# Triangular inverses from blocks of 16, with one more merging level, in a two-layer flow-matching step

## The chip, the cores and the metric

The kernel runs on one core of one Trainium2 chip. The metric is the device time of one launch in microseconds, the median of several runs. A core has five engines with queues of their own: TensorE for matrix products (PE in the rows, PEld its weight loads), VectorE (DVE), ScalarE (ACT), GpSimd (POOL), and SyncE (SP), which here only issues DMAs. Each engine takes its instructions strictly in the order in which the program emits them.

## The reference

Two layers, with the same weights for both streams, run over 128 context tokens and 256 latent tokens (T = 384 in all, width 1024). A layer mixes tokens by a gated DeltaNet (8 heads, both directions), a gated short convolution, and grouped-query attention, then applies an MLP with a hidden width of 4096. The part that matters here is the DeltaNet solve. For every head and direction a unit lower triangular matrix is inverted (or solved against) per chunk:

```python
diff = gc[..., :, None] - gc[..., None, :]
decay = jnp.where(incl, jnp.exp(jnp.where(incl, diff, 0.0)), 0.0)
kb = kc * bc[..., None]
m = jnp.where(strict, jnp.einsum("nbhid,nbhjd->nbhij", kb, kc) * decay, 0.0)
a = m + jnp.eye(C, dtype=f32)
u = lax.linalg.triangular_solve(a, vc * bc[..., None], left_side=True, lower=True)
w = lax.linalg.triangular_solve(a, kb * jnp.exp(gc)[..., None], left_side=True, lower=True)
```

Everything else of a layer is matrix products with float32 weights, norms, gates and softmax.

## The kernel before

**Products.** Each weight block is split into a high and a low part in a reduced float32 type (`wh` by ScalarE, `wl` by VectorE), and each large product runs as three passes (hi·hi, hi·lo, lo·hi), 128x384 or 128x512 at a time, into PSUM tiles named `mm`. Small float32 products go to PSUM tiles named `ax`; the trace records each of those as two instructions, one after the other.

**The inverses (`delta_a`, line 1304).** For one head the kernel forms six 128x128 triangular matrices `M` (two directions, three blocks of 128 tokens). It inverts the 32x32 diagonal blocks of all six at once by substitution on VectorE: 31 steps of a shuffle (`MB<-Mc`), a product (`Pr<-MB,Xc`) and a reduction (`Xc<-Pr`), each step longer than the last. Two levels of block merging on TensorE then give the 128x128 inverse `xe`: 12 products of 32x32 (`ax<-xe,M`), 18 of 32x32 (`ax<-NT`), 6 and 6 of 64x64. These use a part of the array each, so that several can run at once; the text calls them tiled products, and a row of them with nothing else between a run. `delta_b` (line 1433) then uses `xe`. There are 8 heads in each of two layers, so 16 inversions in all.

**The start.** The first layer's modulation vectors come from small products on weights that stream in (`ax<-ws,csil`), a norm needs the column sums of squares (`ax<-sel,sq`), and the first three-pass products follow as soon as the first two blocks of the normed input are there. Products of a matrix of ones with itself (`mm<-ones`, called fillers) stand on TensorE where the planner expects it to idle.

**What sets the order.** The program is first recorded, and `schedule` (line 239) then plans it: each instruction gets a cost from `cost` (line 180) and a priority from its class, and a greedy list scheduler writes the order of every engine. `tiled` (line 162) marks tiled products; leaving tiled mode costs `SWITCH` in the plan. A running balance `bal` of TensorE's work against the share `BUSY` decides on fillers that stand before work that is ready; other fillers fill the plan's idle time. The plan's durations only set the order. On the chip each instruction runs when its engine reaches it and its inputs are there.

Of the kernel before, what the change touches and what calls it, by code (L numbers as in the profile page):

```python
# [9 lines left out]
F32 = mybir.dt.float32  # L10
# [3 lines left out]
AX = mybir.AxisListType  # L14
ADD, SUB, MUL = ALU.add, ALU.subtract, ALU.mult

P = 128
# [144 lines left out]

def tiled(op, ins):

    return "tile_position" in op.k or (op.kind == "matmul" and ins[0].ap[0][1] < P)


def shared_port(op, method, outs, ins, tag):
# [11 lines left out]
def cost(op, method, outs, ins, tag):  # L180

    n = max(size(v) for v in outs[:1] + ins)
    ps = any(tag.get(v.tensor.name) in PSUM_TAGS for v in outs + ins)
    if op.eng == "PE":
        n = size(outs[0])
        if tiled(op, ins):
            if "tile_position" in op.k:
                return n * 0.965 + 3 if op.k["tile_position"] == (0, 0) else 27.0
            return 43.0 if n <= 32 else 71.0
        if method == "transpose":  # L190
            return n * 2 / 2.4 + 3
        if ins[0].dtype == F32R and n >= 256:
            return n / 2.4 + 13.8
        return max(214.0, n * 4 / 2.4 + 3)
    if op.eng == "ACT":
        c = 51 + n * 0.833 + (0 if ps else 42)
        c += 93 * sum(isap(op.k.get(x)) for x in ("bias", "scale")) + 93 * (method == "mul")
        return c + (93 if "accum_out" in op.k else 0)
    if op.eng == "DVE":
        if method == "reciprocal":  # L200
            return 69 + 6.25 * n
        fast = method in ("tensor_scalar", "tensor_copy") and not ps
        sc = sum(isap(op.k.get(x)) for x in ("scalar", "scalar1", "scalar2"))
        return 69 + n * 1.042 * (0.5 if fast else 1) + 58 * sc
    if op.eng == "POOL":
        if method == "memset":
            return 35 + n * 0.833
        if method == "affine_select":
            return 160 + n * 0.83
        if method == "tensor_copy":  # L210
            return 250 if n <= 96 else 345
        return (165 + n * 2.1) if op.k.get("op") != ALU.pow else 300 + 165 * n
    return max(56.0, n * outs[0].shape[0] * 4 / 385.0)
# [15 lines left out]


WINDOW = 3413.0
SWITCH = 63.0
FILL_MARGIN = 100.0
BUSY = 0.4
CREDIT = 600.0
URGENT = {"crit": 1, "step": 1, "crit2": 1, "step2": 1}


def schedule(rec, par):
# [48 lines left out]
            enable(o)  # L288
    for tg in list(queue):
        grant(tg)  # L290
    done, mode = 0, False
    port = bal = last = 0.0
    order = []
    while done < len(ops):
        best = None
        for e in engs:
            t = now[e]
            while future[e] and future[e][0][0] <= t:
                r, p, i = heapq.heappop(future[e])
                heapq.heappush(avail[e], (p, i))  # L300
            if avail[e]:
                c = (t, e)
            elif future[e]:
                c = (future[e][0][0], e)
# [5 lines left out]
        t, e = best  # L310
# [7 lines left out]
        if e == "PE" and warm and warm[0].end is not None:  # L318

            f = warm[0]  # L320
            while True:
                t0 = pe_end
                c = f.cost * slowness(t0)
                if t0 < f.end or t0 + c > t - FILL_MARGIN:
                    break
                g = copy.copy(f)
                g.start, g.end, g.i = t0, t0 + c, o.i
                order.append(g)
                win[1] += g.stream
                bal = min(CREDIT, bal + f.stream * (1 - BUSY))  # L330
                pe_end = t0 + c
            if bal < 0 and o.stream < 0.5 * o.cost and t < par["thin"] and f.end <= t:

                t0 = max(pe_end, t)
                g = copy.copy(f)
                g.start, g.end, g.i = t0, t0 + f.cost * slowness(t0), o.i
                order.append(g)
                win[1] += g.stream
                bal += f.stream * (1 - BUSY)
                now[e] = pe_end = g.end  # L340
                heapq.heappush(avail[e], (p, i))
                continue
# [22 lines left out]
        if e == "SP":  # L365
            if len(flight) >= 8:
                t = o.start = max(t, flight[-8] + 908)
            hw = max(t, hw) + 475
            now[e] = hw - 25
            dma = max(dma, hw + 1800) + o.cost  # L370
            o.end = dma
            flight.append(dma)
        else:
            c = o.cost * slow
            if o.port:
                c += max(0.0, port - t)
                port = t + c
            if e == "PE":
                c += SWITCH * slow * (mode and not o.tiled)
                mode = o.tiled  # L380
                pe_end = t + c
                if o.cls == "fill":
                    o.end = t + c
                    warm.append(o)
                elif warm and warm[0].last is o:
                    warm.pop(0)
                bal = min(CREDIT, bal + o.stream - BUSY * (t + c - last))
                last = t + c
                win[1] += o.stream
            o.end = now[e] = t + c  # L390
# [47 lines left out]
def build(tc, aps):  # L438
# [23 lines left out]
    def axtile():  # L462
        return pax.tile([P, 512], F32, tag="ax", name="ax")
# [6 lines left out]
    sel2 = const.tile([P, 2], F32, name="sel2")  # L470
    sel = const.tile([P, 3, 3], F32, name="sel")
    delta = const.tile([P, 2, 32], F32, name="delta")
    rc = const.tile([P, 2, P], F32, name="rc")
    rs = const.tile([P, 2, P], F32, name="rs")
    mhalf = const.tile([P, 1], F32, name="mhalf")
# [152 lines left out]
    def X(fn, *a):  # L628
        items.append(((), lambda _: fn(*a)))
# [146 lines left out]
    def late_consts():  # L776
        for t_, n_ in ((cdn, "cdn"), (utri, "utri"), (ltri, "ltri"), (delta, "delta"), (rc, "rc"), (rs, "rs"),
                       (csc, "csc"), (gdn, "gdn"), (gqc, "gqc")):
            SP.dma_start(t_, aps[n_])
        for t_, n_ in ((alog, "alog"), (dtb, "dtb")):  # L780
            SP.dma_start(t_, aps[n_].partition_broadcast(P))


    def modfinish(l, pieces, sums):
# [340 lines left out]
    def layer(l):  # L1125
# [178 lines left out]
        def delta_a(h):  # L1304
# [42 lines left out]
                DVE.tensor_tensor(out=E[:, d].rearrange("p t f -> p (t f)"), in0=pq[:, :T],  # L1347
                                  in1=E[:, d].rearrange("p t f -> p (t f)"), op=MUL)
            yield
            Mc, Pr = (W(n, [2, 3, 32]) for n in ("Mc", "Pr"))  # L1350
            Xc = W("Xc", [2, 3, 32], 2)
            Mr = W("Mr", [3, 32])
            for q in range(4):
                s = slice(32 * q, 32 * q + 32)
                POOL.tensor_copy(Mr[s, :, ::-1], M[s, 1, :, s])
            for q in range(4):
                s = slice(32 * q, 32 * q + 32)
                POOL.tensor_copy(Mc[s, 0], M[s, 0, :, s])

            DVE.stream_shuffle(out=Mc[:, 1], in_=Mr, mask=list(range(31, -1, -1)))  # L1360
            POOL.tensor_copy(Pr, delta.unsqueeze(2).to_broadcast([P, 2, 3, 32]))
            DVE.tensor_copy(Xc[:, :, :, 0], delta[:, :, 0:1].to_broadcast([P, 2, 3]))
            yield
            for d in range(2):

# [2 lines left out]
                                   pattern=[[0, 3], [sg, P]], channel_multiplier=-sg)  # L1368
            yield
            f6 = lambda v: v.rearrange("p d t c -> p (d t) c")  # L1370
            for i in range(1, 32):
                MB = W("MB", [2, 3, 32], 2)
                DVE.stream_shuffle(out=f6(MB)[:, :, 0:i], in_=f6(Mc)[:, :, 0:i], mask=[i] * 32)
                DVE.tensor_tensor(out=f6(Pr)[:, :, 0:i], in0=f6(MB)[:, :, 0:i], in1=f6(Xc)[:, :, 0:i], op=MUL)
                DVE.tensor_reduce(out=f6(Xc)[:, :, i], in_=f6(Pr)[:, :, 0:i + 1], axis=AX.X, op=ADD)
                yield

            nt = W("NT", [2, 3, P]).rearrange("p d t f -> p (d t f)")
            U1, U2, Xn, Xh = (nt[:, a:b].rearrange("p (t f) -> p t f", t=n)
                              for a, b, n in ((0, 96, 3), (96, 288, 3), (288, 480, 6), (480, 672, 3)))  # L1380
            DVE.transpose(Xn[:, 0:3], Xc[:, 0])
            DVE.transpose(Xn[:, 3:6], Xc[:, 1, :, ::-1])
            Q = [slice(32 * q, 32 * q + 32) for q in range(4)]
            POOL.memset(Xh[Q[0], :, 32:64], 0.0)
            POOL.memset(Xh[Q[3], :, 0:32], 0.0)
            for q in range(4):
# [3 lines left out]
                yield  # L1390
            for d in range(2):
                for q in range(4):
                    POOL.tensor_copy(xe[Q[q], d, :, Q[q]], Xc[Q[q], d, :, ::-1] if d else Xc[Q[q], d])
            yield
            p1 = axtile()
            p1a = p1[:, 0:96].rearrange("p (t f) -> p t f", t=3)
# [269 lines left out]
        if l == 0:  # L1666
            X(warmup)
            X(pre0)
            evacs = [evac_qkv(0, w) for w in (1, 0, 2)] + [evac_mg(f, True) for f in range(3)]
            for q in range(4):  # L1670
                mq = modquarter(q)
                items.extend(mq[:3])
                if q == 0:
                    X(early_consts)
                items.extend(mq[3:])
                for k in (2 * q, 2 * q + 1):
                    X(lambda k=k: make_h(k))
                    if q < 3:
                        X(lambda k=k: norm_x(k + 2))
                if q == 3:  # L1680
                    X(hold)
                    X(late_consts)
                items.extend(firstproducts(q, evacs))
            X(lambda: save_x(om))
        m2 = modlist(l, "B") if l else []
# [265 lines left out]
```

## Time and profile before

| | |
|---|---|
| median of 3 runs | 1961.99 us (1960.59 to 1962.01) |
| the profiled execution | 1958.58 us |
| its span, first to last instruction | 1957.0 us |
| TensorE busy | 1944.6 us (99%) |
| VectorE busy | 1425.2 us (73%) |
| ScalarE busy | 946.1 us (48%) |
| GpSimd busy | 395.9 us (20%) |
| granted TensorE clock, mean | 1.000 |

TensorE's instructions overlap: a 128x384 pass has a duration of about 341 ns in the rows, and the next starts about 174 ns after it. So the distance between two starts tells what a product costs, and the durations do not.

### The profile page before, as it was taken

What the parts mean: (1) busy time and instruction counts of PE and PEld (TensorE: products, weight loads), DVE (VectorE), ACT (ScalarE), POOL (GpSimd) and SP (SyncE); (2) the same over time, 40 slices, a digit from 0 to 9 for tenths busy, and PEclk for the clock granted to TensorE, in tenths of its full rate; (3) what the DMA queues carried; (4) which work ended last, traced back from release to release, by engine and by line L of the source; (5) the groups of instructions that cost most, each with busy time, mean ns of one, the idle gap of its engine ahead of it and who ended that gap; (6) DMA issues with size and microseconds to landing.
All of it is one profiled execution on the core that took longest, in us unless ns stands there. A gap on an engine that the chain in (4) does not pass through costs nothing.

```text
span 1957.0 us, 35787 instructions
## 1 busy us (share of the span) xinstructions
PE 1944.6 (99%) x12938; PEld 1800.1 (92%) x12938; DVE 1425.2 (73%) x4354; ACT 946.1 (48%) x2176; POOL 395.9 (20%) x651
## 2 busy tenths in 40 slices
PE   9999999999999999999999999999999999999998
PEld 7998999999999899789789999999999998898987
DVE  4688899988869688879467989779888645533334
ACT  3566555555433354334246665545554434543432
POOL 0122122222222312013011022222132212110210
PEclk9999999999999999999999999999999999999999
DMA  8532233333336846866554233333333334544352
GB/s 281 176 105 84 99 121 123 117 116 116 109 114 224 288 142 215 236 207 207 158 183 148 76 97 115 116 119 127 117 116 109 112 129 151 199 124 129 127 126 71
DMA packets 133713, 280.40 MB, mean 143 GB/s; under 512 B 11904, under 2 KB 82080, under 8 KB 133536
## 3 DMA queue, kind: packets, MB, share of 16 engines
q1 hardware_dynamic: 133536, 278.12, 43.9%
q8 instruction: 102, 1.67, 0.3%
q14 instruction: 75, 0.61, 0.1%
HBM read 270.66 MB, written 7.42 MB: 142 GB/s over the span
## 4 chain that ended last, share of the span: by engine, by line
PE 92%; DVE 3%; DMA 2%; ACT 1%; issue 1%; POOL 0%; DVEq 0%; ACTq 0%; POOLq 0%
PE mm L1855 77%; PE ax L1855 15%; DMA wr<-in_wmod 1%; DMA wr<-in_wf 1%; DVE macc L1855 1%; DVE wl L1855 1%; ACT wh L1855 0%; DVE q L1855 0%; DVE XT L1855 0%; ACT junk L1855 0%; ACT E L1855 0%; ACT mm L1855 0%; DVE qu L1855 0%; DVE ns L1855 0%; ACT ht L1855 0%
## 5 line engine op out<-in xcount | busy, mean ns | idle before, releaser
L1855 DVE TENSOR_TENSOR wl<-wr,wh 128x1024 fp32r<-128x1024 f32 (+2 forms) x382 | 480.3, 1259 | 295.6 <-ACT wh L1855 289.6
L1855 ACT CAST wh<-wr 128x1024 fp32r<-128x1024 f32 (+2 forms) x382 | 396.3, 1038 | 564.3 <-PE mm L1855 438.0
L1855 PE MATMUL mm<-HL,wh 128*128 128x384 f32 x1648 | 561.8, 341 | 0.0
L1855 PE MATMUL mm<-HH,wh 128*128 128x384 f32 x1648 | 561.4, 341 | 0.0
L1855 PE MATMUL mm<-HH,wl 128*128 128x384 f32 x1648 | 559.5, 340 | 0.0
L1855 PEld LDWEIGHTS mm<-HL,wh 128*128 128x128 f32 x1648 | 309.7, 188 | 6.0 <-issue 3.1
L1855 PEld LDWEIGHTS mm<-HH,wh 128*128 128x128 f32 x1648 | 309.5, 188 | 6.1 <-issue 3.7
L1855 PEld LDWEIGHTS mm<-HH,wl 128*128 128x128 f32 x1648 | 309.8, 188 | 5.3 <-issue 3.3
L1855 DVE SCALAR_TENSOR_TENSOR macc<-wr,csil,macc 128x1024 f32<-128x1024 f32 x98 | 141.3, 1478 | 12.5 <-DMA wr<-in_wmod 12.5
L1855 PE MATMUL mm<-wh,HL 128*128 128x256 f32 (+1 forms) x480 | 140.6, 293 | 0.0
L1855 PE MATMUL mm<-wh,HH 128*128 128x256 f32 (+1 forms) x480 | 138.9, 290 | 1.3 <-DVE k_y L1855 0.7
L1855 PE MATMUL mm<-wl,HH 128*128 128x256 f32 (+1 forms) x480 | 139.9, 292 | 0.2 <-DVE wl L1855 0.2
L1855 DVE TENSOR_TENSOR Pr<-MB,Xc 128x6 f32<-128x6 f32 (+30 forms) x496 | 138.7, 280 | 0.2
L1855 DVE TENSOR_REDUCE Xc<-Pr 128x6 f32<-128x12 f32 (+30 forms) x496 | 127.1, 256 | 8.1
L1855 DVE STREAM_SHUFFLE MB<-Mc 128x6 f32<-128x6 f32 (+30 forms) x496 | 132.0, 271 | 0.0
L1855 PE MATMUL mm<-al,wh 128*128 128x384 f32 x384 | 130.7, 340 | 0.0
L1855 PE MATMUL mm<-ah,wl 128*128 128x384 f32 x384 | 130.5, 340 | 0.0
L1855 PE MATMUL mm<-ah,wh 128*128 128x384 f32 x384 | 130.0, 339 | 0.0
L1855 PE MATMUL mm<-wh,u 128*128 128x512 f32 x384 | 122.7, 396 | 0.0
L1855 PE MATMUL mm<-wh,ah 128*128 128x512 f32 x288 | 112.9, 392 | 0.0
L1855 PE MATMUL mm<-wl,ah 128*128 128x512 f32 x288 | 112.6, 391 | 0.0
L1855 PE MATMUL mm<-wh,al 128*128 128x512 f32 x288 | 112.6, 391 | 0.0
(278 smaller groups left out, 3304.1 us busy)
## 6 DMA issues: line engine op xcount, KB each, us to landing
wr<-in_wf SPq DMA_DIRECT2D x330, 512.0 KB, 3.3
wr<-in_wmod SPq DMA_DIRECT2D x80, 512.0 KB, 4.3
wr<-in_wq SPq DMA_DIRECT2D x16, 512.0 KB, 3.2
wr<-in_wdg SPq DMA_DIRECT2D x16, 512.0 KB, 3.3
ws<-in_wmod SPq DMA_DIRECT2D x16, 384.0 KB, 6.4
E<-scr SPq DMA_DIRECT2D x16, 384.0 KB, 3.7
Qe<-scr SPq DMA_DIRECT2D x16, 256.0 KB, 3.9
wr<-in_wkv SPq DMA_DIRECT2D x8, 408.0 KB, 3.9
```

The source lines that it names most:

```text
L1855: o.call(*o.a, **o.k)
```

## The change

Substitution stops at blocks of 16: 15 steps instead of 31. Each 32x32 block is now held as two 16x16 blocks stacked on the partitions, picked by two masks `hsel`. One more level of merging on TensorE puts two inverses of 16 together into one of 32: 24 products of 32x32, a copy by ScalarE, 24 more, and an addition on VectorE; all operands lie in a new tile `Rp`. In the planner the costs of tiled products and of leaving tiled mode get new numbers, told apart by the kind of tiled product, and the balance behind fillers is kept against a share of 0.2 instead of 0.4.

```diff
 def tiled(op, ins):
-    return "tile_position" in op.k or (op.kind == "matmul" and ins[0].ap[0][1] < P)
+    return 1 if "tile_position" in op.k else 2 if op.kind == "matmul" and ins[0].ap[0][1] < P else 0
...
-            return 43.0 if n <= 32 else 71.0
+            return 11.0 if n <= 32 else 42.0
...
-SWITCH = 63.0
+SWITCH = {0: 0.0, 1: 63.0, 2: 190.0}
 BUSY = 0.4
+THIN = 0.2
...
-                bal = min(CREDIT, bal + f.stream * (1 - BUSY))
+                bal = min(CREDIT, bal + f.stream * (1 - THIN))
...
-                c += SWITCH * slow * (mode and not o.tiled)
+                c += 0.0 if o.tiled else SWITCH[mode] * slow
...
-                bal = min(CREDIT, bal + o.stream - BUSY * (t + c - last))
+                bal = min(CREDIT, bal + o.stream - THIN * (t + c - last))
...
-            Mc, Pr = (W(n, [2, 3, 32]) for n in ("Mc", "Pr"))
+            rp = W("Rp", [4, 192])
+            F, D, N, Dn = (rp[:, j].rearrange("p (d t c) -> p d t c", d=2, t=3) for j in range(4))
+            Mc, Pr, Xs = (W(n, [2, 3, 16]) for n in ("Mc", "Pr", "Xs"))
...
+            for d in (1, 0):
+                DVE.tensor_scalar(out=Pr[:, d], in0=F[:, d, :, 16:32], scalar1=m1, scalar2=None, op0=MUL)
+                x, y, z = F[:, d, :, 0:16], Pr[:, d], Mr if d else Mc[:, 0]
+                if d:
+                    x, y = x[:, :, ::-1], y[:, :, ::-1]
+                DVE.scalar_tensor_tensor(out=z, in0=x, scalar=m0, in1=y, op0=MUL, op1=ADD)
...
-            for i in range(1, 32):
-                MB = W("MB", [2, 3, 32], 2)
-                DVE.stream_shuffle(out=f6(MB)[:, :, 0:i], in_=f6(Mc)[:, :, 0:i], mask=[i] * 32)
...
+            for i in range(1, 16):
+                MB = W("MB", [2, 3, 16], 2)
+                DVE.stream_shuffle(out=f6(MB)[:, :, 0:i], in_=f6(Mc)[:, :, 0:i], mask=[i] * 16 + [16 + i] * 16)
...
+            for d in range(2):
+                x = Xs[:, d, :, ::-1] if d else Xs[:, d]
+                for b, m in enumerate((m0, m1)):
+                    DVE.tensor_scalar(out=D[:, d, :, 16 * b:16 * b + 16], in0=x, scalar1=m, scalar2=None, op0=MUL)
+            for d in range(2):
+                DVE.transpose(Dn[:, d], D[:, d])
...
+                        PE.matmul(p0a[Q[q], d, t], lhsT=N[Q[q], d, t], rhs=D[Q[q], d, t], start=True, stop=True)
+            ACT.copy(F, p0a)
...
+                        PE.matmul(p0b[Q[q], d, t], lhsT=Dn[Q[q], d, t], rhs=F[Q[q], d, t], start=True, stop=True)
+            DVE.tensor_tensor(out=Xc, in0=p0b, in1=D, op=ADD)
```

On TensorE in the start of the program, before, after the first blocks of the input have been turned (`mm<-ident,XT`), the nine small products for the norm stand one by one between fillers (`mm<-ones`):

```order
L1855 MATMUL mm<-ident,XT 128x128 x2
L1855 MATMUL mm<-ones 128x128 x5
L1855 MATMUL ax<-sel,sq 128x3
L1855 MATMUL mm<-ones 128x128 x5
L1855 MATMUL ax<-sel,sq 128x3
L1855 MATMUL mm<-ones 128x128 x4
L1855 MATMUL ax<-sel,sq 128x3
```

In the changed kernel the same place on TensorE, to the broadcast of the norm (`ax<-ident,np_y`), reads:

```order
L1896 MATMUL mm<-ident,XT 128x128 x2
L1896 MATMUL mm<-ones 128x128
L1896 MATMUL ax<-sel,sq 128x3 x3
L1896 MATMUL mm<-ident,XT 128x128 x2
L1896 MATMUL ax<-sel,sq 128x3 x3
L1896 MATMUL ax<-ws,csil 32x256
L1896 MATMUL ax<-sel,sq 128x3 x3
L1896 MATMUL ax<-ws,csil 32x256 x7
L1896 MATMUL mm<-ident,XT 128x128 x8
L1896 MATMUL ax<-ws,csil 32x256 x3
L1896 MATMUL mm<-ones 128x128 x2
L1896 MATMUL ax<-ident,np_y 128x128 x3
```

The norm's products have moved ahead and modulation products stand among them. Up to the first three-pass product the program now has 34 fillers instead of 56; all later stages keep theirs.

On TensorE in the first head's inversion, the changed kernel has the new level between passes of a weight block (`mm<-HH,wh` and so on) and an attention product (`ax<-KTA,OT`):

```order
L1896 MATMUL mm<-HL,wh 128x384
L1896 MATMUL ax<-Rp 32x32 x12
L1896 MATMUL mm<-HH,wl 128x384
L1896 MATMUL ax<-Rp 32x32 x12
L1896 MATMUL ax<-KTA,OT 128x384
L1896 MATMUL mm<-HH,wh 128x384
L1896 MATMUL ax<-Rp 32x32 x24
L1896 MATMUL mm<-HL,wh 128x384
```

All eight heads of both layers look alike (in one the first 24 stand as 8 and 16, in one the last 24 as 11 and 13). The later levels keep their runs, so that a head has nine runs of tiled products where it had six: 145 runs of 32x32 and 64x64 products in the whole program where it had 98, and 1248 products of 32x32 where it had 480. No other kind of product on TensorE changes its number, but for the fillers.

## Rows read from the trace of the kernel before

**Rows 1.** The page: busy time, share of the span and instructions of each engine.

```profile
PE 1944.6 (99%) x12938; PEld 1800.1 (92%) x12938; DVE 1425.2 (73%) x4354; ACT 946.1 (48%) x2176; POOL 395.9 (20%) x651
```

**Rows 2.** Waits of TensorE: what waited for whom; us in total, times, longest.

```profile
PE ax L1855 <- DVE macc L1855: 2.5, 2, 2.0
PE ax L1855 <- DVE q L1855: 1.1, 3, 0.4
PE mm L1855 <- POOL sel L1855: 1.1, 1, 1.1
PE mm L1855 <- DVE k_y L1855: 0.7, 1, 0.7
PE mm L1855 <- DVE kn L1855: 0.6, 1, 0.6
```

**Rows 3.** Both mixer stages: length, busy per engine, clock, DMA share, GB/s.

```profile
96.00:665.00 569.00, 567.73 (x4162) 541.77 (x4162) 489.70 (x1802) 301.34 (x780) 143.57 (x262) 1.00 0.38 128
...
1041.00:1630.00 589.00, 588.28 (x4283) 566.20 (x4283) 467.73 (x1789) 315.86 (x817) 131.44 (x262) 1.00 0.34 114
```

**Rows 4.** TensorE in order of time, one tiled product: start, us, what, records.

```profile
234.28 0.34 PE L1855 MATMUL mm<-ah,wh 128*128 128x384 f32 x1
...
234.80 0.34 PE L1855 MATMUL mm<-ah,wh 128*128 128x384 f32 x1
235.07 0.24 PE L1855 MATMUL ax<-xe,M 32*32 32x32 f32 x2
235.24 0.44 PE L1855 MATMUL mm<-al,wh 128*128 128x384 f32 x1
235.52 0.34 PE L1855 MATMUL mm<-ah,wl 128*128 128x384 f32 x1
235.70 0.34 PE L1855 MATMUL mm<-ah,wh 128*128 128x384 f32 x1
```

**Rows 5.** The same view of TensorE, a run of 18 tiled products.

```profile
239.38 0.34 PE L1855 MATMUL mm<-al,wh 128*128 128x384 f32 x1
239.65 0.52 PE L1855 MATMUL ax<-NT 32*32 32x32 f32 x36
240.10 0.44 PE L1855 MATMUL mm<-ah,wl 128*128 128x384 f32 x1
240.37 0.34 PE L1855 MATMUL mm<-ah,wh 128*128 128x384 f32 x1
240.55 0.34 PE L1855 MATMUL mm<-al,wh 128*128 128x384 f32 x1
```

**Rows 6.** The same view of TensorE, the start of the program.

```profile
10.56 1.28 PE L1855 MATMUL mm<-ones 128*128 128x128 f32 x10
11.68 0.28 PE L1855 MATMUL ax<-sel,sq 128*128 128x3 f32 x2
...
18.60 0.28 PE L1855 MATMUL ax<-sel,sq 128*128 128x3 f32 x2
...
27.57 0.59 PE L1855 MATMUL mm<-HH,wh 128*128 128x384 f32 x2
```

**Rows 7.** VectorE in order of time, the start of the program.

```profile
11.92 0.56 DVE L1855 TENSOR_TENSOR sq<-sq 128x384 f32<-128x384 f32 x1 [0.27 <-ACT sq L1855]
...
18.92 0.16 DVE L1855 TENSOR_SCALAR n_sx<-ax 128x3 f32<-128x3 f32 x1 [1.23 <-PE ax L1855]
```

**Rows 8.** The start in a stretch of 5 us, columns as in Rows 3.

```profile
15.00:20.00 5.00, 5.00 (x41) 4.37 (x40) 1.12 (x2) 1.66 (x2) 0.83 (x1) 1.00 1.09 364
```

**Rows 9.** Groups of VectorE, the substitution: count, busy us, mean ns, idle before.

```profile
L1855 DVE TENSOR_TENSOR Pr<-MB,Xc 128x6 f32<-128x6 f32 (+30 forms) x496 | 138.7, 280 | 0.2
L1855 DVE STREAM_SHUFFLE MB<-Mc 128x6 f32<-128x6 f32 (+30 forms) x496 | 132.0, 271 | 0.0
L1855 DVE TENSOR_REDUCE Xc<-Pr 128x6 f32<-128x12 f32 (+30 forms) x496 | 127.1, 256 | 8.1
```

**Rows 10.** Groups of ScalarE and VectorE nearest to the new copy and transposes.

```profile
L1855 ACT COPY NT<-ax 128x96 f32<-128x96 f32 (+1 forms) x64 | 16.2, 254 | 12.3 <-PE ax L1855 11.7
L1855 DVE STREAM_TRANSPOSE NT<-Xc 128x96 f32<-128x96 f32 x32 | 7.0, 255 | 0.2
```

More of the change, by code (lines that the diff above doesn't have):

```diff
@@ L290, in schedule @@
         grant(tg)
-    done, mode = 0, False
+    done, mode = 0, 0
     port = bal = last = 0.0
@@ L338, in schedule @@
                 win[1] += g.stream
-                bal += f.stream * (1 - BUSY)
+                bal += f.stream * (1 - THIN)
                 now[e] = pe_end = g.end
@@ L472, in build @@
     delta = const.tile([P, 2, 32], F32, name="delta")
+    d16, hsel = delta[:, :, 0:16], const.tile([P, 2], F32, name="hsel")
     rc = const.tile([P, 2, P], F32, name="rc")
@@ L781, in late_consts, with half_consts @@
             SP.dma_start(t_, aps[n_].partition_broadcast(P))
+    def half_consts():
+        DVE.tensor_reduce(out=hsel, in_=d16, axis=AX.X, op=ADD)
+        DVE.tensor_tensor(out=d16, in0=d16, in1=delta[:, :, 16:32], op=ADD)
     def modfinish(l, pieces, sums):
@@ L1349, in delta_a @@
             yield
-            Mc, Pr = (W(n, [2, 3, 32]) for n in ("Mc", "Pr"))
+            rp = W("Rp", [4, 192])
+            F, D, N, Dn = (rp[:, j].rearrange("p (d t c) -> p d t c", d=2, t=3) for j in range(4))
+            Mc, Pr, Xs = (W(n, [2, 3, 16]) for n in ("Mc", "Pr", "Xs"))
             Xc = W("Xc", [2, 3, 32], 2)
[L1352 to L1362, printed above, removed]
+            Mr = W("Mr", [3, 16])
+            m0, m1 = hsel[:, 0:1], hsel[:, 1:2]
+            for d in (1, 0):
+                for q in range(4):
+                    s = slice(32 * q, 32 * q + 32)
+                    POOL.tensor_copy(F[s, d], M[s, d, :, s])
+            for d in (1, 0):
+                DVE.tensor_scalar(out=Pr[:, d], in0=F[:, d, :, 16:32], scalar1=m1, scalar2=None, op0=MUL)
[3 more added lines that the diff above has]
+                DVE.scalar_tensor_tensor(out=z, in0=x, scalar=m0, in1=y, op0=MUL, op1=ADD)
+            DVE.stream_shuffle(out=Mc[:, 1], in_=Mr, mask=list(range(15, -1, -1)) + list(range(31, 15, -1)))
+            POOL.tensor_copy(Pr, d16.unsqueeze(2).to_broadcast([P, 2, 3, 16]))
+            DVE.tensor_copy(Xs[:, :, :, 0], d16[:, :, 0:1].to_broadcast([P, 2, 3]))
+            POOL.memset(N[:, 0, :, 16:32], 0.0)
+            POOL.memset(N[:, 1, :, 0:16], 0.0)
+            ACT.mul(N[:, 0, :, 0:16], F[:, 0, :, 0:16], m1)
+            ACT.mul(N[:, 1, :, 16:32], F[:, 1, :, 16:32], m0)
             yield
@@ L1370, in delta_a @@
             f6 = lambda v: v.rearrange("p d t c -> p (d t) c")
-            for i in range(1, 32):
-                MB = W("MB", [2, 3, 32], 2)
-                DVE.stream_shuffle(out=f6(MB)[:, :, 0:i], in_=f6(Mc)[:, :, 0:i], mask=[i] * 32)
-                DVE.tensor_tensor(out=f6(Pr)[:, :, 0:i], in0=f6(MB)[:, :, 0:i], in1=f6(Xc)[:, :, 0:i], op=MUL)
-                DVE.tensor_reduce(out=f6(Xc)[:, :, i], in_=f6(Pr)[:, :, 0:i + 1], axis=AX.X, op=ADD)
-                yield
+            for i in range(1, 16):
+                MB = W("MB", [2, 3, 16], 2)
+                DVE.stream_shuffle(out=f6(MB)[:, :, 0:i], in_=f6(Mc)[:, :, 0:i], mask=[i] * 16 + [16 + i] * 16)
+                DVE.tensor_tensor(out=f6(Pr)[:, :, 0:i], in0=f6(MB)[:, :, 0:i], in1=f6(Xs)[:, :, 0:i], op=MUL)
+                DVE.tensor_reduce(out=f6(Xs)[:, :, i], in_=f6(Pr)[:, :, 0:i + 1], axis=AX.X, op=ADD)
+                yield
+            for d in range(2):
[4 more added lines that the diff above has]
+                DVE.transpose(Dn[:, d], D[:, d])
+            p0 = axtile()
+            p0a, p0b = (p0[:, 192 * j:192 * j + 192].rearrange("p (d t c) -> p d t c", d=2, t=3) for j in range(2))
+            Q = [slice(32 * q, 32 * q + 32) for q in range(4)]
+            for d in range(2):
+                for t in range(3):
+                    for q in range(4):
+                        PE.matmul(p0a[Q[q], d, t], lhsT=N[Q[q], d, t], rhs=D[Q[q], d, t], start=True, stop=True)
+            ACT.copy(F, p0a)
+            yield
+            for d in range(2):
+                for t in range(3):
+                    for q in range(4):
+                        PE.matmul(p0b[Q[q], d, t], lhsT=Dn[Q[q], d, t], rhs=F[Q[q], d, t], start=True, stop=True)
+            DVE.tensor_tensor(out=Xc, in0=p0b, in1=D, op=ADD)
+            yield
             nt = W("NT", [2, 3, P]).rearrange("p d t f -> p (d t f)")
@@ L1381, in delta_a @@
             DVE.transpose(Xn[:, 0:3], Xc[:, 0])
-            DVE.transpose(Xn[:, 3:6], Xc[:, 1, :, ::-1])
-            Q = [slice(32 * q, 32 * q + 32) for q in range(4)]
+            DVE.transpose(Xn[:, 3:6], Xc[:, 1])
             POOL.memset(Xh[Q[0], :, 32:64], 0.0)
@@ L1392, in delta_a @@
                 for q in range(4):
-                    POOL.tensor_copy(xe[Q[q], d, :, Q[q]], Xc[Q[q], d, :, ::-1] if d else Xc[Q[q], d])
+                    POOL.tensor_copy(xe[Q[q], d, :, Q[q]], Xc[Q[q], d])
             yield
@@ L1682, in layer @@
                     X(late_consts)
+                    X(half_consts)
                 items.extend(firstproducts(q, evacs))
```

## The prediction

> **What bounds the kernel now.** I read the page's busy times first. TensorE is busy for 1944.6 of 1957.0 us, VectorE for 73%, the others for less [rows 1]. A busy TensorE need not be a working one, so the waits come next. In the whole span nine pairs make it wait; the five longest, shown, come to 6.0 us, and each of the other four is at most 0.6 [rows 2]. The two stages that hold all the inversions run from 96 to 665 us and from 1041 to 1630 us: TensorE is busy for 567.73 of 569 us and for 588.28 of 589, at a granted clock of 1.00, while VectorE is busy for 489.70 and 467.73 us [rows 3]. VectorE is loaded there, but always in time. Last I looked at distances between TensorE's starts, since a wait shorter than an instruction's own duration would hide in "busy". In the stretch shown three passes take 0.52 us from 234.28 to 234.80 [rows 4], 0.173 us each, and the last two passes of [rows 5] keep that step. So nothing is hidden: in the mixer stages the time is the sum of what TensorE is given to do. An instruction added on TensorE is paid in full, and one taken from VectorE saves nothing.
>
> **What leaves VectorE.** 16 of 31 steps go in each of 16 heads, 256 steps of three instructions. All 496 steps cost 138.7 + 132.0 + 127.1 = 397.8 us [rows 9], and the later steps are the longer ones, so at least 16/31 of that, 205 us, goes. What comes in per head is eleven instructions (two masks, two sums, four placings, two transposes, one addition); at the 0.255 us of a nearby transpose [rows 10] that is 2.8 us a head, 45 us in all. VectorE gets about 160 us lighter. This can shorten the run only where TensorE waits for it: at most the four rows of 2.5 + 1.1 + 0.7 + 0.6 = 4.9 us [rows 2], with at most 0.6 in any row not shown. The 2.5 is a wait for `macc`, the modulation sums, and the others are for `q`, `k_y` and `kn`, small steps of the attention and key path that pass by latency; none waits for the substitution. I count zero, with 4.9 kept for the range.
>
> **What TensorE gets.** 768 products of 32x32, two trace records each, and 47 more runs of tiled products. The price of a run is read where one stands in an even stream of passes. A run of one: the start of the pass ahead of it is 234.80 and that of the third pass behind it 235.70 [rows 4], 0.90 us where three steps take 0.52, so the run costs 0.38 us. A run of 18: from 239.38 to 240.55 is 1.17 us [rows 5], so 0.65. Seventeen products more cost 0.27 us, 0.016 each, and what is left is 0.36 us for a run as such. The rows show where this sits: the tiled products start 0.27 us behind the pass ahead of them instead of 0.173, and the second pass behind them also comes late, 0.28 us behind the first [rows 4, 5]. The new runs do the same kind of product on the same diagonal places as the 18, so I take this price for them: 47 x 0.36 = 16.9 us and 768 x 0.016 = 12.3 us, 29.2 us together, half in either mixer stage. From both sides: at the lower end the 24-runs pack better and some runs stand beside other small products, 25 us; at the upper end each product costs the average of the 18-run with its surcharge, 0.65/18 = 0.036 us, 27.7 us, with about the half of 16.9 again, 36 us. I stay with 29.2 because both rows are the same operation in the same surroundings.
>
> The planner's new numbers are a cost for order alone. They put a run of 18 at 18 x 0.011 + 0.190 = 0.39 us where the row has 0.65 [rows 5]; TensorE will be behind its plan in the mixers, so the producers are early and its other inputs are ready.
>
> The page "TensorE: Matmul & The Clock Gate" of the Trainium skill (section "Wait — 56ns, not 53.3ns?") says that start-to-start distances never fall under about 25 ns however few columns a product has. The row here has 36 records in a run that is 0.65 us dear in all [rows 5], 0.45 us from its first start to the next pass, under 13 ns a record, so for products on separate parts of the array the trace differs and decides. By the page alone the 1536 new records would be an estimated 38 us in place of 12.3, and the sum 26 us higher.
>
> **New waits.** The chain of the new level passes TensorE, ScalarE (the copy of 128x192, by its nearest row 0.254 us [rows 10]) and TensorE again, then VectorE. In the first head only an attention product and one pass stand between the second 12 products and the 24 that need the copy. TensorE executes in order, so if the copy is late, the next passes queue behind it and everything waits. Where it is in time this costs nothing; where all 16 heads wait for the length of a copy and its signals, some 0.5 us, it is 8 us. The present levels have the same hand-over (`U1`, by that same copy row) and no row of them is among the shown waits, so I count zero and keep 0 to 8. The other added work (masks and zeros on GpSimd and ScalarE) lies ahead of this chain on engines that are busy for 20% and 48% [rows 1]; without that cover it delays the chain and is the same bound.
>
> **The start.** TensorE is busy from the first microseconds, but with fillers. VectorE ends the last sum of squares at 11.92 + 0.56 = 12.48 us, and TensorE takes it only at 18.60 [rows 6, 7]: 6.1 us late, in its own queue behind fillers. The norm follows at 18.92 and the first three-pass product at 27.57. Five fillers take 11.68 - 10.56 = 1.12 us [rows 6], 0.224 each, and the 22 that go are 4.9 us. Since modulation products fill the places between, the first three-pass product should start near 22.5. Could something else be late then? The weights: between 15 and 20 us the DMA engines are full at 364 GB/s [rows 8], and the later weight loads wait for buffers that TensorE frees. An earlier TensorE frees them earlier, but a full DMA side could take back part or all. Bounds: 0 and 6.1 us gained; I take 4.9, the work that is gone.
>
> **The sum.** 1958.6 (profiled) + 29.2 - 4.9 = 1982.9 us. The median of the runs, 1962.0, is 3.4 us above the profiled execution, so I forecast 1986 us, 1.2% slower.
>
> **Rivals.**
>
> *The relief pays after all, not slower.* The 0.36 us per run might be a wait for operands rather than the price of changing the array's use; with a lighter VectorE operands would be early and it would vanish. Then the new products cost 12.3 us, the start gives 4.9 and VectorE's waits 4.9: 1964.5 us, no change by measure; it gets faster only if the products fall below 0.0128 us each as well. For it: VectorE is the second busiest engine. Against it: the two runs shown have the same delays, 0.27 ahead and 0.28 behind, to the hundredth of a microsecond, which waits for different producers would not have. It decides from a run price under about 0.05 us on. 4%, with 2% for faster.
>
> *The planner's price is right.* 768 x 0.011 + 47 x 0.19 = 17.4 us; with the start 1974.5. Only if the rows I read are dearer than the usual ones. 8%.
>
> *The start gives nothing back, or the clock falls.* Fewer fillers leave TensorE thinner before 27 us; the rows of the start show 1.00 throughout [rows 8], so there is no row for a thin start. At half of that, 1.2 instead of 2.4 GHz, some microseconds of products would double, at most about the 6 us just gained. 1991 if nothing is gained, 1995 with a fall on top. 13%. [...]
>
> *The new chain holds TensorE up.* 8 us at the upper bound, 1994. 9%.
>
> *The floor per start holds for tiled products.* 26 us more, 2012 us. 1%.
>
> **How the numbers follow.** The forecast as worked out has 65%, with its own range of 1981 to 1991 (tiled work 25 to 33 us, the start 3 to 6). The eight-in-ten range runs from 1977 to 1994: it reaches into the two rivals of the start and the chain and most of the way to the planner's price. What a measurement can tell from no change is about 0.2%, 3.9 us, so from 1966 on it is slower. Faster 0.02, same 0.03, slower 0.95.
>
> **What would show it.** In the changed kernel's profile: VectorE near 1265 us busy; TensorE without new waits; both mixer stages about 14.5 us longer; a run of 12 costing 0.55 us and one of 24 costing 0.75 by distances of starts; the first three-pass product near 22.5 us. I am wrong if the runs of `Rp` cost half of that, if TensorE waits for the copy in each head, or if the mixer stages get shorter while TensorE had no wait to lose.

## The result, and the profile after

The changed kernel takes 1983.8 us (median of 4 runs, 1983.63 to 1984.17) against 1961.29 us of the kernel before (4 runs, 1959.1 to 1962.01): ratio 1.0120, 95% interval 1.0107 to 1.0133, slower by 22.5 us by the medians and 23.5 by the ratio. The profiled execution takes 1983.7 us with a span of 1981.7; its span is 24.7 us longer than that of before.

The page's busy line of the changed kernel, which answers to [rows 1]:

```profile
PE 1967.2 (99%) x14430; PEld 1807.6 (91%) x14430; DVE 1277.3 (64%) x3508; ACT 957.4 (48%) x2224; POOL 398.9 (20%) x683
```

VectorE lost 147.9 us of busy time and the kernel got slower: TensorE has 1492 more records and 22.6 us more busy time. The two mixer stages between the same marks of the program (to about 0.1 us), which answer to [rows 3] (length, busy time of each engine, clock, DMA share, GB/s):

```profile
90.30:674.00 583.70, 582.05 (x4925) 548.33 (x4924) 415.08 (x1378) 307.66 (x803) 144.69 (x278) 1.00 0.39 125
1051.00:1654.80 603.80, 602.03 (x5051) 572.96 (x5051) 394.40 (x1366) 320.46 (x841) 133.72 (x278) 1.00 0.35 111
```

The first starts 5.7 us earlier than in the kernel before and is 14.7 us longer, the second is 14.8 us longer. TensorE is as full as it was. These three numbers are nearly the whole result: -5.7 + 14.7 + 14.8 = 23.8 us of the 24.7; about 1 us more comes between the stages.

The waits of TensorE, which answer to [rows 2] (us in total, times, longest):

```profile
PE ax L1896 <- POOL xe L1896: 1.7, 3, 0.7
PE ax L1896 <- DMA wr<-in_wmod: 1.4, 1, 1.4
PE ax L1896 <- DVE macc L1896: 1.2, 1, 1.2
...
PE mm L1896 <- DVE wl L1896: 1.0, 2, 0.8
```

All its waits sum to 9.9 us, where those of before sum to 7.2. None is for ScalarE's copy in the new chain. New are three waits for `xe`, GpSimd's copies of the finished 32x32 inverses, and one for a block of modulation weights; the wait for `wl` was 0.2 us before.

TensorE in order of time in the changed kernel, two runs of 12 and one of 24 of the new products (start, us, what, records; two records a product), which answer to [rows 4, 5]:

```profile
253.09 0.42 PE L1896 MATMUL mm<-ah,wh 128*128 128x384 f32 x1
253.44 0.39 PE L1896 MATMUL ax<-Rp 32*32 32x32 f32 x24
253.76 0.44 PE L1896 MATMUL mm<-al,wh 128*128 128x384 f32 x1
254.04 0.34 PE L1896 MATMUL mm<-ah,wl 128*128 128x384 f32 x1
254.21 0.34 PE L1896 MATMUL mm<-ah,wh 128*128 128x384 f32 x1
...
254.91 0.34 PE L1896 MATMUL mm<-al,wh 128*128 128x384 f32 x1
255.18 0.62 PE L1896 MATMUL ax<-Rp 32*32 32x32 f32 x48
255.73 0.45 PE L1896 MATMUL mm<-ah,wl 128*128 128x384 f32 x1
256.01 0.34 PE L1896 MATMUL mm<-ah,wh 128*128 128x384 f32 x1
256.19 0.35 PE L1896 MATMUL mm<-al,wh 128*128 128x384 f32 x1
...
1229.94 0.34 PE L1896 MATMUL mm<-al,wh 128*128 128x384 f32 x1
1230.21 0.39 PE L1896 MATMUL ax<-Rp 32*32 32x32 f32 x24
1230.53 0.44 PE L1896 MATMUL mm<-ah,wl 128*128 128x384 f32 x1
1230.81 0.34 PE L1896 MATMUL mm<-ah,wh 128*128 128x384 f32 x1
1230.98 0.34 PE L1896 MATMUL mm<-al,wh 128*128 128x384 f32 x1
```

Read as in the prediction, the run of 24 costs 256.19 - 254.91 - 3 x 0.1735 = 0.76 us (forecast 0.75). For a run of 12 the forecast was 0.55. The upper one reads 254.21 - 253.09 - 0.52 = 0.60 us, but another small product (`ax<-ident,od`) stands just ahead of its first pass. In the rows from 1229.94 on there are only passes around the run, and it costs 1230.98 - 1229.94 - 0.52 = 0.52. Of 18 runs of 12 with passes next to them, the eight that stand like this one all cost 0.52; the other ten, with a small product or another run just one pass ahead, read 0.60 to 0.63, because they start 0.35 to 0.37 us behind the pass ahead instead of 0.27. Two such runs together cost 1.05 us, so 0.52 each is the price.

The start, on TensorE, which answers to [rows 6], and two stretches of it, as in [rows 8]:

```profile
11.70 0.83 PE L1896 MATMUL ax<-sel,sq 128*128 128x3 f32 x6
...
15.59 0.83 PE L1896 MATMUL ax<-ident,np_y 128*128 128x128 f32 x6
...
21.02 0.60 PE L1896 MATMUL mm<-HH,wh 128*128 128x384 f32 x2
```
```profile
10.00:15.00 5.00, 5.00 (x46) 3.26 (x45) 1.54 (x6) 2.87 (x7) 0.87 (x1) 1.00 1.10 346
15.00:20.00 5.00, 5.00 (x46) 4.24 (x44) 3.10 (x11) 2.49 (x5) 0.00 (x0) 1.00 1.10 350
```

The last sums of squares are taken at 11.70 instead of 18.60 us and the first three-pass product starts at 21.02 instead of 27.57, 6.6 us earlier, with the clock at 1.00 and the DMA engines full.

The substitution, as in [rows 9]:

```profile
L1896 DVE STREAM_SHUFFLE MB<-Mc 128x6 f32<-128x6 f32 (+14 forms) x240 | 50.4, 217 | 0.0
L1896 DVE TENSOR_TENSOR Pr<-MB,Xs 128x6 f32<-128x6 f32 (+14 forms) x240 | 50.2, 209 | 0.2
L1896 DVE TENSOR_REDUCE Xs<-Pr 128x6 f32<-128x12 f32 (+14 forms) x240 | 49.9, 208 | 3.7
```

256 of 496 steps are gone, and with them 247 of 398 us of records.

### The profile page after: what moved, and what is told of

Same layout as the page of the kernel before. It is cut to its first block, busy times and chain, and to the rows that moved or that the text cites. A ratio compares the mean times of both kernels' runs of the same rounds, so it can differ in the third digit from the quotient of the medians.

```text
span 1981.7 us, 38090 instructions
## 1 busy us (share of the span) xinstructions
PE 1967.2 (99%) x14430; PEld 1807.6 (91%) x14430; DVE 1277.3 (64%) x3508; ACT 957.4 (48%) x2224; POOL 398.9 (20%) x683
## 4 chain that ended last, share of the span: by engine, by line
PE 93%; DVE 3%; ACT 1%; DMA 1%; POOL 1%; issue 1%; DVEq 0%; ACTq 0%; POOLq 0%; SPq 0%
PE mm L1896 77%; PE ax L1896 16%; DMA wr<-in_wf 1%; DVE macc L1896 1%; DVE wl L1896 0%; POOL xe L1896 0%; DVE q L1896 0%; DMA wr<-in_wmod 0%; DMA gqb<-in_gqb 0%; DVE XT L1896 0%; ACT wh L1896 0%; ACT junk L1896 0%; POOL NT L1896 0%; ACT mm L1896 0%; POOL Rp L1896 0%
## 5 line engine op out<-in xcount | busy, mean ns | idle before, releaser
L1896 PEld LDWEIGHTS mm<-wh,HH 128*128 128x128 f32 x480 | 90.9, 190 | 3.9 <-issue 1.4
L1896 PEld LDWEIGHTS mm<-wl,HH 128*128 128x128 f32 x480 | 91.2, 190 | 1.7 <-DVE wl L1896 0.4
L1896 PEld LDWEIGHTS mm<-wh,HL 128*128 128x128 f32 x480 | 91.2, 190 | 1.7 <-issue 1.2
```

The lines of the kernel that those rows point to most:

```text
L1896: o.call(*o.a, **o.k)
```

## The experiments

The theory: TensorE is full, so the kernel pays for the new products (some 29 us) and gets back the fillers of the start (some 5). The rivals: the lighter VectorE matters, the new chain holds TensorE up, or the planner's numbers decide more than the start. All ratios are against the kernel before, run beside each, with 95% intervals. There its median was 1958.6 to 1959.6 us, and 1961.29 beside the changed kernel, so differences between two of these kernels are best read from the ratios.

**planner_alone**: the kernel before with the new planner numbers only.

```diff
-            return 43.0 if n <= 32 else 71.0
+            return 11.0 if n <= 32 else 42.0
...
+SWITCH = {0: 0.0, 1: 63.0, 2: 190.0}
+THIN = 0.2
```

> The inverses of before, with the planner's new numbers and filler share. The plan has 130 fillers instead of 152, all 22 of them gone from the start, and 100 runs of tiled products instead of 98. My theory (TensorE pays for each run 0.36 us, for each tiled product 0.016 us, and is otherwise without gaps): the start gives back 5 to 6 us, the two runs cost 0.7, so 1956 us against 1961.3 before. Rival (the start is bound by the weight transfers, or the clock falls): 1961 us or more.

1955.58 us, ratio 0.9981 (0.9972 to 0.9990). The mixer starts 5.7 us earlier, as in the changed kernel, but the span ends only 2.5 us earlier: waits for `xe` (2.5 us) and for `wl` (1.7) came in. The new numbers are a small gain by themselves, by the ratio 3.7 us where some 5 were expected.

**inverse_alone**: the new inverses with the old planner numbers.

> The new inverses with the planner's old numbers: 768 more products of 32x32 and 137 runs instead of 98, fillers as before. My theory: 768 x 0.016 + 39 x 0.36 = 26.3 us, so 1987.6 us. Rival (the planner's own price of 0.011 per product and 0.19 per run): 15.9 us, 1977 us. Rival (a lighter VectorE pays): under 1975 us.

1997.44 us, ratio 1.0193 (1.0178 to 1.0208), 10 us over the expectation. The waits show where: for `xe` TensorE waits 9.4 us, in 12 places. So a term that the prediction had put at zero exists, 1.7 us in the changed kernel and much more with the old numbers. It is taken up below.

**half_steps**: the kernel before, with half of the substitution left out.

```diff
+            POOL.memset(Xc.rearrange("p d t c -> p (d t) c")[:, :, 16:32], 0.0)
-            for i in range(1, 32):
+            for i in range(1, 16):
```

> The kernel before with the last 16 of the 31 substitution steps left out (their columns are set to zero by GpSimd), so that part of the inverse is not computed; VectorE is some 200 us lighter and TensorE has the same products in 96 runs instead of 98. My theory: VectorE's time is worth nothing, 1960.5 us, within 0.2% of before. Rival (the relief pays where TensorE waits for VectorE): 1956 us or less.

1959.9 us, ratio 1.0001 (0.9992 to 1.0011). Its busy line:

```profile
PE 1944.9 (99%) x12938; PEld 1798.4 (92%) x12938; DVE 1251.8 (64%) x3330; ACT 946.9 (48%) x2176; POOL 399.8 (20%) x667
```

VectorE is 173 us lighter than in [rows 1], TensorE is the same, and so is the time. The relief is worth nothing that the interval, some 2 us to either side, can tell.

**no_new_products**: the changed kernel without the 768 products and their copy.

```diff
-                        PE.matmul(p0a[Q[q], d, t], lhsT=N[Q[q], d, t], rhs=D[Q[q], d, t], start=True, stop=True)
-            ACT.copy(F, p0a)
-                        PE.matmul(p0b[Q[q], d, t], lhsT=Dn[Q[q], d, t], rhs=F[Q[q], d, t], start=True, stop=True)
-            DVE.tensor_tensor(out=Xc, in0=p0b, in1=D, op=ADD)
+            DVE.tensor_tensor(out=Xc, in0=Dn, in1=D, op=ADD)
```

> The changed kernel without the 768 products of the new level and the copy between them (the two halves of the block inverse are added up without their product, so that part of the inverse is not computed). 130 fillers and 96 runs. My theory: what is left of the change is the start, so the time of the planner's numbers alone, 1955 us, give or take 2. Rival (the lighter VectorE is worth something that the new products hid): under 1951 us.

1955.95 us, ratio 0.9983 (0.9974 to 0.9992). Its span, 1952.8 us, is 28.9 us under that of the changed kernel, and by the ratios the difference is 0.0137, 27 us (some 24 to 30 with both intervals): the forecast term of 29.2 us, measured by itself. Everything else in the change together is a gain of about 3 us by the ratio, 4 by the spans.

**one_run**: the changed kernel, where products wait in the program for all inputs of their group, so that a group stands in one run; 99 runs instead of 145.

```diff
-                        PE.matmul(p0a[Q[q], d, t], lhsT=N[Q[q], d, t], rhs=D[Q[q], d, t], start=True, stop=True)
+                        o = PE.matmul(p0a[Q[q], d, t], lhsT=N[Q[q], d, t], rhs=D[Q[q], d, t], start=True, stop=True)
+                        for c in pl:
+                            o.deps.setdefault(c, False)
...
+                    for c in cp:
+                        o.deps.setdefault(c, False)
```

> The changed kernel with the same 1248 products of 32x32, but the first 24 of the new level wait in the plan for both directions, and the first 12 of the next level for all eight copies into xe, so that each stands as one run: 99 runs instead of 145. My theory: 46 x 0.36 = 16.6 us back, 1967 us, more by what TensorE then waits for the last copy. Rival (the price of a run is a wait for its operands, which a later and longer run does not shorten): 1984 us or more. Rival (the planner's 0.19 per run): 1975 us.

1965.38 us, ratio 1.0030 (1.0019 to 1.0041): 17.6 us less than the changed kernel by the ratios, 18.4 by the medians, for 46 runs with the same products, so 0.38 to 0.40 us each. Some 2.7 us of it are waits that went (TensorE's waits sum to 7.2 us instead of 9.9; for `xe` it waits once, 0.6 us), which leaves 0.32 to 0.34. The price of a run as such (0.36 from [rows 4, 5]) holds within that when runs are taken away, and it is the larger part of what the new level costs. The Trainium skill ("TensorEngine Tiling (Array Packing)", section "Key Properties") says that a change of the tiling mode drains TensorE; it gives no price. A fixed price of a run fits that, but no run here shows what TensorE does in that time.

**products_twice**: the changed kernel, each new product issued twice.

```diff
-                for t in range(3):
+                for t in range(6):
+                    t %= 3
```

> The changed kernel with each product of the new level executed twice in the same run: 768 products more, 137 runs instead of 145. My theory: 1983.8 + 768 x 0.016 - 8 x 0.36 = 1993.2 us. Rival (the price is one per run, however long): 1981 us. Rival (a floor of 25 ns per recorded start): 1983.8 + 38 - 3 = 2019 us.

2003.79 us, ratio 1.0221 (1.0206 to 1.0237): 10 us over the expectation. A run of 48 there, in order of time:

```profile
259.12 0.34 PE L1898 MATMUL mm<-ah,wh 128*128 128x384 f32 x1
259.39 1.02 PE L1898 MATMUL ax<-Rp 32*32 32x32 f32 x96
260.34 0.45 PE L1898 MATMUL mm<-al,wh 128*128 128x384 f32 x1
260.62 0.34 PE L1898 MATMUL mm<-ah,wl 128*128 128x384 f32 x1
260.80 0.35 PE L1898 MATMUL mm<-ah,wh 128*128 128x384 f32 x1
```

260.80 - 259.12 - 0.52 = 1.16 us, so 24 products more cost 0.40 us, 0.017 each: the price per product holds inside an even run. But only 7 of the 24 runs of 48 are as short as this one, 0.95 us from their first start to the next pass; the other 17 are longer, by 5.6 us together. The waits hold a row that the changed kernel does not have, and a longer one for `macc`:

```profile
PE ax L1898 <- issue: 3.3, 6, 1.1
PE ax L1898 <- DVE macc L1898: 3.0, 3, 1.3
```

The 3.3 us put down to "issue" are idle time inside six of the long runs, a part of their 5.6. The start gained 2.7 us less, with the clock at half from 13.6 to 17.0 us, and `macc` holds TensorE for 1.8 us more. Together that is about the 10 us. Why long runs stretch is not shown; the fifteen runs of 24 in the changed kernel are all equally long.

**inverse_scalar_copies**: inverse_alone, with the copies into `xe` on ScalarE.

```diff
-                    POOL.tensor_copy(xe[Q[q], d, :, Q[q]], Xc[Q[q], d])
+                    ACT.copy(xe[Q[q], d, :, Q[q]], Xc[Q[q], d])
```

> The new inverses with the planner's old numbers, with the eight copies into xe by ScalarE instead of GpSimd; 135 runs instead of 137. The run with the copies on GpSimd took 1997.4 us, 10 more than I had worked out, and shows 9.4 us of TensorE waiting for those copies. Theory (the copies hold TensorE up): about 9 us back, 1988 us. Rival (the waits only move, to the next hand-over): 1995 us or more.

1997.92 us, ratio 1.0196 (1.0179 to 1.0213), the time of inverse_alone. TensorE still waits for `xe`, 5.9 us in place of 9.4, now for ScalarE, and VectorE's `wl` is 1.8 us late. But the clock differs too: the mean is 0.995 or 0.996 in all four executions, where inverse_alone has 0.998 to 1.000. The stretches at half (columns as in [rows 3]):

```profile
321.60:328.40 6.80, 6.80 (x82) 4.53 (x80) 0.00 (x0) 3.34 (x14) 0.64 (x3) 0.50 0.08 30
389.90:393.30 3.40, 3.40 (x54) 2.34 (x54) 0.00 (x0) 1.57 (x7) 0.00 (x0) 0.50 0.00 0
451.30:458.10 6.80, 6.43 (x90) 4.68 (x90) 0.00 (x0) 2.80 (x12) 0.18 (x1) 0.50 0.02 4
```

From 321.60 to 328.97 us TensorE does ten passes and five runs, which by the rows at full clock (0.1735 us a pass, 0.38 to 0.70 a run) cost 4.7 us, in 7.4. At that rate the 17 us at half cost some 6 to 7, an estimate. So the faster copies may have given back most of the 9 us expected, and the clock took it again; this run can't tell. It does show that the wait does not belong to GpSimd alone, so the plan was the next suspect: it tells TensorE to be at a place before its inputs are there.

**measured_prices** and **old_prices**: the changed kernel, with only the planner's prices of tiled products replaced. A run of 24 is planned at 0.45 us in the changed kernel, at 0.74 in the first of these and at 1.10 in the second; the trace has 0.76.

```diff
-            return 11.0 if n <= 32 else 42.0
+            return 16.0 if n <= 32 else 56.0
...
-SWITCH = {0: 0.0, 1: 63.0, 2: 190.0}
+SWITCH = {0: 0.0, 1: 63.0, 2: 360.0}
```

This is measured_prices; old_prices has 43.0 and 71.0 for the products and 63.0 for a run in these places.

> The changed kernel with the planner's prices of tiled products set to what its own trace shows: 16 and 56 ns a product and 360 ns for the first of a run, in place of 11, 42 and 190 (a run of 24 is then planned at 0.74 us, where the rows show 0.757; the change plans it at 0.45, and the numbers before the change at 1.10). 143 runs of tiled products. Theory, that the waits for the copies into xe come with a planned time that is longer than the real one: with the plan at the rows, TensorE waits little for xe, 1 to 4 us in all, and the time is that of the changed kernel, 1984, plus or minus 3. Rival, that any dearer price brings them: waits for xe near the 9.4 us of inverse_alone, and 1990 to 1997.

> The changed kernel with nothing but the planner's prices of tiled products put back: 43 and 71 ns a product and 63 ns for a run, in place of 11, 42 and 190. The fillers (130) and the balance stay new; 136 runs of tiled products, nine fewer than in the changed kernel, worth 9 x 0.36 = 3.2 us. Theory, that a planned price above the row (1.10 against 0.757 us for a run of 24) lets TensorE run ahead of its plan and makes it wait for the copies into xe: waits for xe of 6 to 12 us in all and 1988 to 1993 us (1983.8 - 3.2 + some 8 more of waits in the records and in the passes that hide them). Rival, that the waits of inverse_alone came from its old fillers and balance: waits for xe of 1 to 3 us, and 1980 to 1984.

measured_prices: 1986.72 us, ratio 1.0153 (1.0136 to 1.0170), against 1.0120 (1.0107 to 1.0133): no difference that these intervals settle. old_prices: 1995.29 us, ratio 1.0186 (1.0169 to 1.0203), 11.5 us over the changed kernel by the medians and 12.9 by the ratios, with nine runs fewer. The waits of the two for `xe`, measured_prices first:

```profile
PE ax L1896 <- POOL xe L1896: 2.4, 4, 1.0
```
```profile
PE ax L1896 <- POOL xe L1896: 9.9, 17, 1.2
```

With the fillers and the balance held fixed, the price alone makes the waits come and go in this kernel. The reading that fits is that TensorE, planned too dear, runs ahead of its plan and meets the copies before they are done, and planned at or under the real price comes late and finds them there. The price alone is not enough everywhere: the kernel before has the same old prices, which put its run of 18 at 0.84 us where [rows 5] have 0.65, and no wait for `xe`. old_prices also loses clock, in all its runs (mean 0.996 to 0.997): in the profiled execution three stretches of 13.6 us in all stand at 0.50, each behind a wait of 1.2 us, which by the estimate above cost some 5 us. So about half of the loss is waits (8.2 us more for `xe`, less 3.2 for nine runs) and half is clock. One of the places, in windows and then in order of time (the bracket is the idle time ahead and what ended it):

```profile
1538.00:1540.00 2.00, 1.33 (x25) 0.88 (x25) 0.00 (x0) 0.24 (x1) 1.32 (x6) 0.99 0.07 27
1540.00:1546.00 6.00, 6.00 (x71) 4.59 (x70) 0.21 (x1) 3.37 (x11) 0.00 (x0) 0.50 0.01 3
1546.00:1548.00 2.00, 2.00 (x14) 1.75 (x12) 1.01 (x1) 0.85 (x3) 0.00 (x0) 0.80 0.00 0
1548.00:1550.00 2.00, 2.00 (x17) 2.00 (x17) 0.35 (x1) 1.57 (x6) 0.00 (x0) 1.00 0.88 262
```
```profile
1538.67 0.25 PE L1896 MATMUL ax<-xe,M 32*32 32x32 f32 x4 [1.21 <-POOL xe L1896]
```

The wait of 1.21 us ends at 1538.67, and from about 1540 to 1546 the clock is 0.50, with TensorE busy all the time.

**old_inverse_one_run** and **fewest_runs**: the inverses of before with the new planner numbers, and the products of the next level held until all copies into `xe` are there (65 runs of tiled products instead of 100); fewest_runs also issues the modulation products of two weight blocks in one run.

```diff
-                    POOL.tensor_copy(xe[Q[q], d, :, Q[q]], Xc[Q[q], d, :, ::-1] if d else Xc[Q[q], d])
+                    cp.append(POOL.tensor_copy(xe[Q[q], d, :, Q[q]], Xc[Q[q], d, :, ::-1] if d else Xc[Q[q], d]))
...
+                    for c in cp:
+                        o.deps.setdefault(c, False)
```

> The inverses of before with the planner's new numbers, the first 12 products of a head's merging in one run behind all eight copies, and the modulation products of two weight blocks in one run: 65 runs of tiled products instead of 100, and 46 instead of 54 of the modulation's. My theory: 1955.6 - 35 x 0.36 - 8 x 0.36 = 1940 us, more by what TensorE waits for the last copy. Rival (the price is a wait): 1955 us.

> The inverses of before with the new planner numbers, and the products of p1a of a chunk held back until all its copies into xe are there, so that they stand in one run: 65 runs in place of 100 (and 53 of the modulation, which fewest_runs had down to 46). Theory, 0.36 us for each run and nothing else: planner_alone less 35 x 0.36 = 12.6 us, so 1943. fewest_runs, with the modulation merged as well, measured 1943.28 and had its clock at half for 3.4 us in the start. Rival, that holding the products back makes TensorE wait for the copies into xe: waits of 3 us or more for xe, and 1946 to 1950.

fewest_runs: 1943.28 us, ratio 0.9914 (0.9900 to 0.9929). old_inverse_one_run: 1943.1 us, ratio 0.9922 (0.9907 to 0.9936). Both beat the two kernels of this study. Against planner_alone the second gains 0.0059 by the ratios, 11.6 us for 35 runs, 0.33 us each, of which 2.8 us in all are waits that went (TensorE's waits sum to 7.8 us instead of 10.6). So runs of the old products have a price too, of the same kind and some 0.25 to 0.33 us. Merging the modulation products adds nothing measurable; the profile of fewest_runs shows waits of 3.5 us for `macc` (2.1 in the other) and a start at less than full clock:

```profile
10.00:15.00 5.00, 5.00 (x41) 3.42 (x39) 1.53 (x5) 2.91 (x7) 0.87 (x1) 0.82 1.11 341
15.00:20.00 5.00, 5.00 (x38) 3.39 (x36) 1.31 (x5) 1.26 (x3) 0.00 (x0) 0.84 1.10 351
```

## Why the prediction was right, step by step

**The bound** was right: TensorE has no gaps to lose, so its added work is paid in full. half_steps shows the other half of it, that 173 us less on VectorE change nothing.

**VectorE** was forecast at 1265 us and is at 1277.3. The steps that went and the eleven instructions that came were near their sizes in records (247 us gone, at least 205 forecast; the eleven cost 45.7 us, 45 forecast); the busy time, which counts overlapping records once, fell by 148 instead of 160. Nothing hung on it.

**The new products** were forecast at 29.2 us. By no_new_products they cost 28.9 by the spans and 27 by the ratios, and 14.5 us in either mixer stage became 14.7 and 14.8. The rows add up to the same: thirty runs of 12 at 0.52 us, fifteen of 24 at 0.76 and four of 8 to 16 products at about 0.5 are 29 us, an estimate. The two prices held apart too, if less sharply than they were read: 0.32 to 0.40 us for a run by one_run and 0.25 to 0.33 by old_inverse_one_run, where 0.36 was taken, and 0.017 us for a product by the run of 48. One reading was a little off: in [rows 5] the second pass comes 0.27 us behind the first and not 0.28, so the two runs do not agree "to the hundredth of a microsecond". Nothing in the sum hangs on it.

**The waits** were put at zero, with the reason that TensorE would be behind its plan. The reason fits what the runs show and was worth more than was seen: with the old prices in the plan the same kernel takes 11.5 us more, in waits and in clock. What was wrong is the place that was watched. The bounds were given for ScalarE's copy `F`, for which TensorE never waits by any row; the copies into `xe`, one step later, cost 1.7 us in the changed kernel and 9.9 with the old prices.

**The start** was forecast at 4.9 us and gave 6.6 at the first three-pass product and 5.7 at the mixer. The fillers that went give 4.9. Another 1.3 us come from the first 19 fillers, which take 6.13 us instead of 7.46: their pace rises from 7 to 11 records a microsecond at 4.5 us in this execution and at 7.3 in that of before. There the traces' record of the clock begins, at 1.00; the clock column of the windows, which reads 1.00 from the first microsecond, knows nothing of the time ahead of it. This moment lies between 4.0 and 6.9 us in the profiled executions of the other kernels, all with the same 19 fillers, so I do not count it to the change.

**The sum** by spans was 24.3 us and is 24.7. The forecast of 1986 lies 2.2 us above the result of 1983.8 mainly through one term: the 3.4 us by which the median of the runs lay above the profiled execution of before was carried over, and the profiled execution of the changed kernel lies 0.1 us from its median. Those 3.4 us were scatter between executions, and no property of the program: beside the experiments the median of the kernel before is 1958.6 to 1959.6 us.

**The rivals.** The relief of VectorE fell by half_steps, the planner's price (17.4 us) by no_new_products and by the run of 24 at 0.76 us, and the floor for a start by the run of 96 records that costs 1.16 us, 12 ns each. A fall of the clock in the start is no part of the result, but it is real: it stands in the profiles of fewest_runs and products_twice, two of the nine profiles with the new start, and in none of the four with the old one. That the missing fillers bring it is not shown. The hold-up of TensorE by the new chain did not come at its place.

Open: why long runs stretch in products_twice; what the copies on ScalarE are worth at full clock; and why waits of the same length go with a falling clock in old_prices and leave the profiled execution of inverse_alone at 1.000.

## What to carry to other kernels

Where TensorE has no gaps, price a change by what it puts on TensorE, however much it takes off another engine, and count the runs of small products as well as the products: here 47 runs cost some 15 to 17 us of the 27 to 29, by the prices above, more than the 768 products in them. Merging small products into fewer runs is then worth more than making the work around them lighter. A planner's prices are part of the kernel: in this one a price above the real one made TensorE arrive before its inputs, though the same prices did not in the kernel before.

## What the runs showed of the hardware

A wait of 1.2 us amid thin tiled products was followed, 1.3 us later, by some 6.8 us at a granted clock of 0.50, while TensorE was busy all the time (old_prices, the windows above); in inverse_scalar_copies the same follows waits of 1.56 us at 321.4 and 450.6 us. So more time can go at such a place than the wait itself; that the wait brings the fall is not shown, since inverse_alone waits for `xe` up to 1.5 us at a mean clock of 1.000.

The scatter between executions of one kernel can go with the granted clock: the four of measured_prices have mean clocks of 1.000, 0.999, 0.998 and 0.997 and spans of 1983.3, 1983.7, 1986.1 and 1989.4 us. It need not: half_steps has spans of 1956.7 to 1960.6 us at 1.000, and 1960.6 at 0.998.
